# A decayed cumulative sum of x @ w: half of w's first quarter goes to GpSimd's queue, other first parts, and a float32 warm-up

## The chip, the cores and the metric

The kernel runs on one core of a Trainium2 chip. The metric is the device time of one launch in microseconds; lower is better. A core has TensorE (PE, matrix products), VectorE (DVE), ScalarE (ACT), GpSimd (POOL) and SyncE (SP), each with its own program, and 16 DMA engines that carry the transfers which SP, ACT and POOL issue.

## The reference

x has 16 batches of 2048 steps and 1024 features, w is 1024 x 1024, decay has 1024 values, all float32:

```python
xw = x @ w
out[:, 0, :] = xw[:, 0, :]
for t in range(1, S):
    out[:, t, :] = decay[None, :] * out[:, t - 1, :] + xw[:, t, :]
```

## The kernel before

**Tiling.** x is cut into 64 chunks of 512 steps (TL), four to a batch. A chunk is loaded by four DMAs, one for each quarter of the features (`load`, L105); each goes to 32 partitions, and GpSimd's queue turns float32 into bfloat16 on the way. A chunk has 16 blocks of 32 steps (NJ); a DMA may load some of the blocks only. VectorE transposes 32 x 32 blocks of pairs of bfloat16 (`turn`, L115, from `xb` to `xw`), so that the features lie on the partitions and each pair of neighbouring features is interleaved; ScalarE or VectorE pull the pairs apart (`part`, L123, to `xt`). Products can read the pairs straight from `xw` or the copies in `xt`. A product (L131) takes 128 features (k = 0 to 7) and 128 output columns (n = 0 to 7). Even k are the even rows of w (e = 0), odd k the odd ones (e = 1). The result in PSUM is scanned along the steps by VectorE (L229, or L210 on pairs that ScalarE and GpSimd have combined), transposed back (L266) and stored by SP (L290).

**Order.** Every engine's program follows the order of the lines, since each instruction is pinned. An agenda written by hand names deeds by letters; the string under -99 is the start, which the change touches:

- `M0` to `M3` (`load_half`): the loads of chunk 0's two parts and chunk 1's two parts. `cuts` says how many blocks a part has: chunk 0 has 9 and 7 (H is 8), chunk 1 has 8 and 8.
- `load_w` (L307): w is loaded in quarters (h: half of the columns, e: even or odd rows), each by four DMAs, one for each 32 partitions. Quarter (0, 0) goes in float32 over SP's and ACT's queues before all else; `U0` to `U2` (`load_part`) send the others over GpSimd's queue as bfloat16. They land in two `ot` tiles that are used for storing only later.
- `W` on VectorE, `w` on ScalarE (`settle`, L314): the copies of w into `wsb`, four for each quarter: 0 to 3 of (0, 0), 4 to 7 of (0, 1), and so on.
- `E` (transposes of a part, in four pieces), `F` and `G` (pulling the pairs apart on VectorE and ScalarE), `D` (decay's columns).
- `K0` to `K3` (`spin_on`, L348): warm-up products that wait for x. ScalarE copies one value of each quarter of x's first part into a gate matrix, and TensorE then multiplies with it.

**TensorE's start.** After a memset of `idle` it makes 22 products of zeros in bfloat16 (L332, 128 x 512), then 3, 3, 3 and 1 products with the four gates. Then come the products of chunk 0, part by part, four n at a time, even k from `xw` first, then odd k from `xt`; then those of chunk 1, its first blocks and then the rest; then whole chunks.

**GpSimd's queue.** Eight DMAs can be on their way at a time: each issue waits for the landing of the one eight before it. Order of the issues: `M0`, `U0`, `M1`, `M2`, `M3`, `U1`, `U2`, then chunk 2 and 3 of x (the deeds `L`). GpSimd also makes additions (L205, L254) between issues.

The lines for the start, as far as words don't tell them:

```python
    load_w((nc.sync, nc.scalar), 0, 0)
    pin(nc.vector.memset(idle, 0.0))
    ...
    spin(22, idle[:, 0:128])
    H = NJ // 2
    cuts = (((0, H + 1), (H + 1, NJ)), ((0, H), (H, NJ)))
    ...
    def spin_on(q):
        pin(nc.scalar.copy(out=gates[q][quad(q), 0:1], in_=xb_of[0][quad(q), 0, 0:1]))
        spin(3 if q < NQ - 1 else 1, gates[q])
```

Of the kernel before, what the change touches and what calls it, by code (L numbers as in the profile page):

```python
# [9 lines left out]
FP32 = mybir.dt.float32  # L10
BF16 = mybir.dt.bfloat16
# [3 lines left out]
def _ap(ap_obj: bass.AP, new_ap, extra_offset=0):  # L15
    return dataclasses.replace(
        ap_obj,
        ap=[list(p) for p in new_ap],
        offset=ap_obj.offset + extra_offset,
    )  # L20
# [5 lines left out]
def kernel(  # L26
# [26 lines left out]
    nc = tc.nc  # L53
    pin = tc.keep_in_program_order
    B, S, D = x.shape
    assert w.shape == (D, D)

    NQ = 4
    P = 32
    CQ = D // NQ  # L60
    K = CQ // P
    M = K // 2
    TL = 512
    NJ = TL // P
    NC = S // TL
    R = K // 2
    CH = D // 2
    CR = CH // NQ

    const = ctx.enter_context(tc.tile_pool(name="const", bufs=1))  # L70
# [5 lines left out]
    def ring(pool, name, count, shape, dtype=FP32):  # L76
        i = turns[name] = turns.get(name, -1) + 1
        return pool.tile(shape, dtype, name=f"{name}{i % count}")

    def quad(q):  # L80
        return slice(q * P, (q + 1) * P)
# [12 lines left out]
    def ot_tile(nj):  # L94
        return ring(sb, "ot", 4, [128, nj, CR])

    xb_of = {}
    xw_of = {}
    xt_of = {}
# [25 lines left out]
    def matmul(ps, n, k, xt, t0=0, t1=TL, start=0, pairs=None):  # L125
        if pairs is None:
            rhs = xt[:, k // 2, k % 2, t0:t1]
        else:
            rhs = pairs[:, k // 2, t0 // P:t1 // P, :, k % 2].rearrange("p j i -> p (j i)")
        lhs = wsb[:, k, n].rearrange("p q i -> p (q i)")  # L130
        pin(nc.tensor.matmul(  # L131
            out=ps[:, t0:t1] if ps.shape[1] >= t1 else ps,
            lhsT=lhs,
            rhs=rhs,
            start=(k == 0 and t0 == start),
            stop=(k == K - 1),
        ))
# [3 lines left out]
    class Tile:  # L141
# [45 lines left out]
        def copy(self):  # L187
            self.xs = sb.tile([128, 2 * TL], FP32, name=f"xs{self.lot % 3}")[:, 0:self.T]
            size = self.T // len(self.parts())
            for i, ps in enumerate(self.parts()):  # L190
                pin(nc.scalar.copy(out=self.xs[:, i * size:(i + 1) * size], in_=ps))  # L191
# [82 lines left out]
    class Outlet:  # L274
# [8 lines left out]
        def store(self, b, t0):  # L283
# [4 lines left out]
            for j in range(0, self.nj, nj):  # L288
# [8 lines left out]

    room = [ot_tile(2 * NJ).rearrange("p j c -> p (j c)") for _ in range(2)]
    size = M * CH
    stage = {(0, 0): room[0][:, 0:size],  # L300
             (0, 1): room[0][:, size:size * 3 // 2].bitcast(BF16),
             (1, 0): room[1][:, 0:size // 2].bitcast(BF16),
             (1, 1): room[1][:, size // 2:size].bitcast(BF16)}

    def load_w(queues, h, e):
        for i, q in enumerate((0, 2, 1, 3)):
            pin(queues[i % len(queues)].dma_start(  # L307
                out=stage[h, e][quad(q)].rearrange("p (m d) -> p m d", m=M),
                in_=_ap(w, [[2 * D, P], [2 * P * D, M], [1, CH]],
                        (q * CQ + e) * D + h * CH)))  # L310

    def settle(h, e, m, copy):
        src = stage[h, e][:, m * CH:(m + 1) * CH]
        pin(copy(out=wcols[:, 2 * m + e, h],  # L314
                 in_=src.rearrange("p (q r i) -> p q r i", q=NQ, r=R)))

    idle = const.tile([128, TL], BF16, name="idle")
    spare = ring(psp, "spare", 1, [128, TL])
    rows = const.tile([128, 2, P], FP32, name="rows")
    touch = const.tile([128, 1], BF16, name="touch")  # L320
    load_w((nc.sync, nc.scalar), 0, 0)
    pin(nc.vector.memset(idle, 0.0))  # L322
    pin(nc.vector.memset(rows, 0.0))
    pin(nc.scalar.copy(out=touch, in_=idle[:, 0:1]))

    gates = [const.tile([128, 128], BF16, name=f"gate{q}") for q in range(NQ)]
    for gate in gates:
        pin(nc.vector.memset(gate, 0.0))

    def spin(count, by):  # L330
        for _ in range(count):
            pin(nc.tensor.matmul(out=spare, lhsT=by, rhs=idle, start=True, stop=True))  # L332

    spin(22, idle[:, 0:128])
    H = NJ // 2
    cuts = (((0, H + 1), (H + 1, NJ)), ((0, H), (H, NJ)))
    for q in range(NQ):
        pin(nc.sync.dma_start(
            out=rows[q * P:q * P + R],
            in_=_ap(decay, [[P, R], [CH, 2], [1, P]], q * CR)))  # L340
# [4 lines left out]
            load(i // 2, q, *cuts[i // 2][i % 2])  # L345

    def spin_on(q):
        pin(nc.scalar.copy(out=gates[q][quad(q), 0:1], in_=xb_of[0][quad(q), 0, 0:1]))  # L348
        spin(3 if q < NQ - 1 else 1, gates[q])

    def load_part(i):
        load_w((nc.gpsimd,), *((0, 1), (1, 0), (1, 1))[i])

    def part_one(i, copy):
        part(i // 8, copy, i % 4, i % 4 + 1, *cuts[i // 8][i // 4 % 2])
# [65 lines left out]
    def turn_and_load(c):  # L421
# [38 lines left out]
        "L": lambda i: load(*loads.pop(0)) if loads else None,  # L460
    }
    agenda = {
        -99: "M0 U0 M1 M2 M3 U1 U2 w0 W1 w2 W3 K0 K1 K2 K3 E0 E1 G0 E2 G1 E3 F2 G3 W4 w5 W6 W7 D E4 E5 G4 E6 G5 E7 F6 G7 E8 E9 G8 E10 G9 E11 F10 G11 E12 L E13 G12 L E14 G13 E15 L F14 G15",
        0: "p0 z0 W8 W9 W10 W11",
        1: "g0",
        2: "L S1 L",
# [89 lines left out]
    for step, (g, n) in enumerate(slots):  # L556
        T = TL * len(g)
        left = step - len(slots)
        if n % R == 0:
            ns, nj = range(n, n + R), T // P  # L560
            if left == -2 * R:
                outlets = [Outlet(ns, H, half) for half in range(2)]
            else:
                pieces = 1 if left < -7 * R else 2 if left < -6 * R else nj // H
                outlets = [Outlet(ns, nj, pieces=pieces)]
        if left == -R:
            outlets = []
        if step == 0:
            heads = [ring(psp, "ps", 3, [128, T]) for _ in range(3)]
            firsts = [ps[:, 0:TL] for ps in heads] + [spares[0]]  # L570
            seconds = [ps[:, TL:T] for ps in heads] + [spares[1]]
            for j0, j1 in cuts[0]:
                for e in range(2):
                    for k in range(e, K, 2):
                        for i in range(R):
                            matmul(firsts[i], i, k, xt_of[0], j0 * P, j1 * P, j0 * P,
                                   pairs=None if e else xw_of[0])
            for k0 in range(0, K, 2):
                for i in range(R):
                    for k in (k0, k0 + 1):  # L580
                        matmul(seconds[i], i, k, xt_of[1], 0, H * P,
                               pairs=xw_of[1] if k0 < 4 else None)
            for i in range(R):
                for k in range(K):
                    matmul(seconds[i], i, k, xt_of[1], H * P, TL, H * P,
                           pairs=xw_of[1] if i < 2 else None)
        if step < R:
            ps = heads[n] if n < 3 else tuple(spares)
        else:
            if step == K + 1:  # L590
                ps = nexts
            elif len(g) == 2 or n % R < 3:
                ps = ring(psp, "ps", 3, [128, T])
            else:
                ps = ring(psp, "spare", 1, [128, TL])
            todo = [(k, l) for k in range(K) for l in range(len(g))]
            if step < K:
                todo.sort(key=lambda kl: kl[0] % 2)
            elif step == K:
                todo = []  # L600
                nexts = (ring(psp, "spare", 1, [128, TL]), ring(psp, "ps", 3, [128, T])[:, TL:T])
                for l in range(len(g)):
                    for i, one in enumerate((ps[:, l * TL:(l + 1) * TL], nexts[l])):
                        for k in range(K):
                            matmul(one, n + i, k, xt_of.get(g[l]),
                                   pairs=xw_of[g[l]] if l or not i and k >= M else None)
            elif step == K + 1:
                todo = []
            if left == -1:
                ps = tuple(both[:, t:t + TL // 2] for t, both in zip(  # L610
                    (0, TL // 2), (ps, ring(psp, "ps", 3, [128, TL]))))
                blocks += [bank("spare1", 1), bank("ps", 3)]
                for t, half in zip((0, TL // 2), ps):
                    for k in range(K):
                        matmul(half, n, k, xt_of[g[0]], t, t + TL // 2, t)
                    if not t:
                        cross((1,), (0, 1))
                todo = []
            for k, l in todo:
                matmul(ps[:, l * TL:(l + 1) * TL], n, k, xt_of[g[l]])  # L620
        tiles.append(Tile(g, n, ps, outlets))
        do = agenda.get(step, agenda.get(left) if left >= -20 else None)
        if do is None:
            do = usual(step)
        else:
            do = do.split()
            if left == -20:
                do = rest(step) + do
        perform(do)
# [29 lines left out]
```

## Time and profile before

| what | value |
|---|---|
| median of 3 runs | 905.64 us (904.32 to 905.7) |
| the profiled execution | 905.1 us, of which the span of instructions is 903.3 us |
| PE, DVE, ACT, POOL busy | 99%, 91%, 76%, 73% of the span |
| first warm-up product, first real product | 1.20 us, 10.61 us |
| last product begins | 898.62 us |
| clock granted to TensorE | 1.00 in the record |

The times of a trace are microseconds from the start of its span. A row of a timeline gives start, length, engine, line, operation, tiles (out<-in) and count, and in brackets the idle time of the engine before it with what ended it. PEld is TensorE's loading of weights, which overlaps with products. Products overlap in their ends too, so what one costs is read from the distance of starts: 0.216 us for 512 columns at full clock.

### The profile page before, as it was taken

To read this page: it belongs to the slowest core of one execution; us is meant where nothing else is said; L and a number is where in the kernel's file an instruction comes from. 1 tells how busy PE (TensorE), PEld (TensorE's weight loads), DVE (VectorE), ACT (ScalarE), POOL (GpSimd) and SP (SyncE) were. 2 spreads that over 40 slices of the span, in tenths; PEclk is the share of its full clock that TensorE was granted. 3 is DMA by queue.
4 is the path that set the end of the run, shared out by engine and by line. 5 is a ranking of instruction groups with operands and counts; after the bars stand their busy time and mean duration, and the time that the engine had idled before them with its cause. 6 is when DMAs were issued, how large, how long until landed. Compare 5 with 4: busy or idle time off the path is not lost.

```text
span 903.3 us, 12163 instructions
## 1 busy us (share of the span) xinstructions
PE 896.9 (99%) x4216; PEld 412.8 (46%) x4216; DVE 824.2 (91%) x632; ACT 685.9 (76%) x957; POOL 657.1 (73%) x755
## 2 busy tenths in 40 slices
PE   9999999999999999999999999999999999999998
PEld 5444444444444444444444444444444444444444
DVE  4899998998999999999998999999999999999998
ACT  4899867877877877878778778777787787787743
POOL 7978678877767778777677687777777776876632
PEclk9999999999999999999999999999999999999999
DMA  9999999999999999999999999999999999999858
GB/s 193 184 215 215 223 244 208 215 229 232 248 239 251 253 241 246 250 258 249 241 237 226 222 231 226 232 229 227 233 227 226 233 231 222 227 230 214 184 143 232
DMA packets 403182, 204.77 MB, mean 227 GB/s; under 512 B 9392, under 2 KB 402096, under 8 KB 403120
## 3 DMA queue, kind: packets, MB, share of 16 engines
q1 hardware_dynamic: 265808, 134.77, 60.9%
q0 software_dynamic: 137024, 68.70, 56.4%
q8 instruction: 33, 0.54, 0.2%
q10 hardware_dynamic: 288, 0.52, 0.2%
q14 instruction: 29, 0.24, 0.1%
HBM read 138.42 MB, written 134.22 MB: 302 GB/s over the span
## 4 chain that ended last, share of the span: by engine, by line
PE 92%; DMA 3%; DVE 2%; issue 1%; POOL 1%; ACT 0%; DVEq 0%; POOLq 0%; ACTq 0%
PE ps L131 91%; DMA xb<-in_x_dram 2%; POOL xb L105 1%; DMA ot<-in_w_dram 1%; PE spare L131 1%; DVE so L229 1%; DVE ot L266 0%; DVE so L210 0%; DVE xw L115 0%; POOL xs L205 0%; PE spare L392 0%; PE ps L392 0%; ACT h L171 0%; DVE h L401 0%; POOL so L199 0%
## 5 line engine op out<-in xcount | busy, mean ns | idle before, releaser
L131 PE MATMUL ps<-xt,wsb 128*128 128x512 bf16 (+1 forms) x4024 | 865.6, 378 | 0.4 <-DVE so L229 0.4
L131 PEld LDWEIGHTS <-wsb 128*128 128x128 bf16 x4168 | 407.3, 98 | 479.0 <-issue 1.7
L205 POOL TENSOR_TENSOR xs<-h,xs 128x512 f32<-128x512 f32 (+1 forms) x190 | 242.8, 1278 | 183.1 <-ACT h L171 84.6
L266 DVE STREAM_TRANSPOSE ot<-so 128x1024 f32<-128x1024 f32 (+2 forms) x264 | 300.1, 1175 | 5.7 <-DMA out_dram<-ot 3.6
L191 ACT COPY xs<-ps 128x1024 f32<-128x1024 f32 (+1 forms) x190 | 188.8, 994 | 145.2 <-PE ps L131 141.6
L254 POOL TENSOR_TENSOR so<-h,xs 128x512 f32<-128x512 f32 (+1 forms) x190 | 241.1, 1271 | 48.0 <-ACT h L171 28.1
L123 ACT COPY xt<-xw 128x2048 bf16<-128x2048 bf16 (+3 forms) x136 | 242.1, 1788 | 8.9 <-DVE xw L115 8.9
L105 POOL DMA_DIRECT2D xb<-in_x_dram x264 | 174.2, 661 | 6.7 <-DMA xb<-in_x_dram 3.1
L171 ACT ACTIVATE h<-so,dec 128x512 f32<-128x512 f32 (+1 forms) x190 | 145.3, 765 | 37.3 <-DVE so L210 34.0
L115 DVE STREAM_TRANSPOSE xw<-xb 128x2048 f32<-128x2048 f32 (+3 forms) x78 | 147.4, 1902 | 8.8 <-DMA xb<-in_x_dram 8.8
L210 DVE TENSOR_TENSOR_SCAN so<-spare,keep,xs 128x512 f32<-128x512 f32 (+1 forms) x97 | 119.6, 1236 | 24.1 <-POOL xs L205 23.9
L210 DVE TENSOR_TENSOR_SCAN so<-spare,xs 128x512 f32<-128x512 f32 x93 | 113.2, 1219 | 26.4 <-POOL xs L205 23.5
L171 ACT ACTIVATE h<-ps,dec 128x512 f32<-128x512 f32 (+1 forms) x190 | 129.9, 683 | 0.0
L229 DVE TENSOR_TENSOR_SCAN so<-dec,ps 128x1024 f32<-128x1024 f32 x34 | 76.8, 2261 | 1.0 <-ACT h L171 1.0
L229 DVE TENSOR_TENSOR_SCAN so<-dec,keep,ps 128x1024 f32<-128x1024 f32 (+1 forms) x35 | 75.9, 2169 | 0.0
L258 ACT COPY keep<-so 128x1 f32<-128x1 f32 x136 | 25.3, 189 | 9.6 <-DVE so L229 9.0
L201 ACT COPY so<-keep 128x1 f32<-128x1 f32 x97 | 18.4, 191 | 2.7 <-DVE ot L266 2.5
L131 PE MATMUL ps<-xw,wsb 128*128 128x256 bf16 (+3 forms) x72 | 12.3, 306 | 0.4 <-DVE xw L115 0.4
L131 PE MATMUL spare<-xt,wsb 128*128 128x512 bf16 (+3 forms) x60 | 12.6, 330 | 0.0
L199 POOL MEMSET so<- 128x1 f32 x93 | 10.6, 116 | 0.6 <-DVE ot L266 0.6
L332 PE MATMUL spare<-idle 128*128 128x512 bf16 x22 | 7.4, 515 | 1.2 <-DVE idle L322 1.2
L307 POOL DMA_DIRECT2D ot<-in_w_dram x12 | 6.5, 545 | 1.0 <-issue 0.4
(39 smaller groups left out, 37.9 us busy)
## 6 DMA issues: line engine op xcount, KB each, us to landing
out_dram<-ot SPq DMA_DIRECT2D x236, 512.0 KB, 11.1
xb<-in_x_dram POOLq DMA_DIRECT2D x248, 256.0 KB, 7.9
out_dram<-ot SPq DMA_DIRECT2D x56, 128.0 KB, 2.6
out_dram<-ot SPq DMA_DIRECT2D x8, 256.0 KB, 4.0
ot<-in_w_dram POOLq DMA_DIRECT2D x12, 128.0 KB, 6.1
xb<-in_x_dram POOLq DMA_DIRECT2D x8, 128.0 KB, 4.8
out_dram<-xb SPq DMA_DIRECT2D x3, 256.0 KB
xb<-in_x_dram POOLq DMA_DIRECT2D x4, 144.0 KB, 6.2
```

Of the source, the lines that this page charges most:

```text
L105: pin(nc.gpsimd.dma_start(out=xb_of[c][quad(q), j0:j1], in_=_ap(x, [[D, P], [P * D, j1 - j0], [1, CQ]], (b * S + t0 + j0 * P) * D + q * CQ)))
L115: pin(nc.vector.transpose(out=dst.rearrange("p (m j i) -> p j m i", m=M, i=P)[:, j0:j1, m0:m1], in_=src.rearrange("p (j m c) -> p j m c", ...
L123: pin(copy(out=xt_of[c][:, m0:m1, :, j0 * P:j1 * P], in_=src))
L131: pin(nc.tensor.matmul(out=ps[:, t0:t1] if ps.shape[1] >= t1 else ps, lhsT=lhs, rhs=rhs, start=(k == 0 and t0 == start), stop=(k == K - 1),))
L171: pin(nc.scalar.activation(out=h[:, i * size:(i + 1) * size], in_=src, func=mybir.ActivationFunctionType.Copy, scale=dec[:, self.n:self.n ...
L191: pin(nc.scalar.copy(out=self.xs[:, i * size:(i + 1) * size], in_=ps))
L205: pin(nc.gpsimd.tensor_tensor(out=odds, in0=self.g, in1=odds, op=ALU.add))
L210: pin(nc.vector.tensor_tensor_scan(out=so[:, 3:T + 2:2], data0=squares[-1][:, n:n + 1].to_broadcast([128, T // 2]), data1=self.xs[:, 1:T:2 ...
L229: pin(nc.vector.tensor_tensor_scan(out=so[:, t + 2:t + 2 + size], data0=dec[:, n:n + 1].to_broadcast([128, size]), data1=ps, initial=befor ...
L254: pin(nc.gpsimd.tensor_tensor(out=self.so[:, 2:T + 2:2], in0=self.h, in1=self.xs[:, 0:T:2], op=ALU.add))
L258: pin(nc.scalar.copy(out=self.keep, in_=self.so[:, self.T + 1:self.T + 2]))
L266: pin(nc.vector.transpose(out=outlet.ot[:, :, c0:c0 + P], in_=self.so[:, 2 + t0:2 + t0 + nj * P].rearrange("p (i t) -> p i t", t=P)))
```

## The change

Five things change, all of them before TensorE's steady stream.

- w's quarter (0, 0) is divided. The first two of its four row groups (m = 0 and 1) go in float32 over SP and ACT, as the whole quarter did; the other two (m = 2 and 3) go as bfloat16 over GpSimd's queue in four DMAs of 64 KB, ahead of `M0`. `U0` is now this half, and `U1` to `U3` are the former `U0` to `U2`.
- `cuts`: chunk 0 is loaded, transposed and multiplied in parts of 10 and 6 blocks (before 9 and 7), chunk 1 in parts of 7 and 9 (before 8 and 8). The products of chunk 1 use the same bound (`Q`).
- The order of issues on GpSimd's queue becomes `U0 M0 U1 M1 M2 M3 U2 U3`.
- The 22 bfloat16 warm-up products become 4 products of float32 (128 x 512) on a tile `wide` that VectorE clears.
- Of the gated products only one stays, with the last quarter of x's first part (`K3`).

```diff
-    stage = {(0, 0): room[0][:, 0:size],
-             (0, 1): room[0][:, size:size * 3 // 2].bitcast(BF16),
+    stage = {(0, 1): room[0][:, size:size * 3 // 2].bitcast(BF16),
              (1, 0): room[1][:, 0:size // 2].bitcast(BF16),
              (1, 1): room[1][:, size // 2:size].bitcast(BF16)}
 
-    def load_w(queues, h, e):
+    lead = {0: room[0][:, 0:2 * CH], 2: room[0][:, 2 * CH:3 * CH].bitcast(BF16)}
+
+    def load_w(queues, to, h, e, m0=0, m1=M):
         for i, q in enumerate((0, 2, 1, 3)):
             pin(queues[i % len(queues)].dma_start(
-                out=stage[h, e][quad(q)].rearrange("p (m d) -> p m d", m=M),
-                in_=_ap(w, [[2 * D, P], [2 * P * D, M], [1, CH]],
-                        (q * CQ + e) * D + h * CH)))
+                out=to[quad(q)].rearrange("p (m d) -> p m d", d=CH),
+                in_=_ap(w, [[2 * D, P], [2 * P * D, m1 - m0], [1, CH]],
+                        (q * CQ + 2 * P * m0 + e) * D + h * CH)))
 
     def settle(h, e, m, copy):
-        src = stage[h, e][:, m * CH:(m + 1) * CH]
+        if h or e:
+            src = stage[h, e][:, m * CH:(m + 1) * CH]
+        else:
+            src = lead[m // 2 * 2][:, m % 2 * CH:(m % 2 + 1) * CH]
...
-    idle = const.tile([128, TL], BF16, name="idle")
+    wide = const.tile([128, TL], FP32, name="wide")
+    idle = wide[:, 0:TL // 2].bitcast(BF16)
...
-    load_w((nc.sync, nc.scalar), 0, 0)
-    pin(nc.vector.memset(idle, 0.0))
+    load_w((nc.sync, nc.scalar), lead[0], 0, 0, 0, 2)
+    pin(nc.vector.memset(wide, 0.0))
...
-    gates = [const.tile([128, 128], BF16, name=f"gate{q}") for q in range(NQ)]
-    for gate in gates:
-        pin(nc.vector.memset(gate, 0.0))
-
-    def spin(count, by):
+    gate = const.tile([128, 128], BF16, name="gate")
+    pin(nc.vector.memset(gate, 0.0))
+
+    def spin(count, by, on):
         for _ in range(count):
-            pin(nc.tensor.matmul(out=spare, lhsT=by, rhs=idle, start=True, stop=True))
-
-    spin(22, idle[:, 0:128])
+            pin(nc.tensor.matmul(out=spare, lhsT=by, rhs=on, start=True, stop=True))
+
+    spin(4, wide[:, 0:128], wide)
     H = NJ // 2
-    cuts = (((0, H + 1), (H + 1, NJ)), ((0, H), (H, NJ)))
+    cuts = (((0, H + 2), (H + 2, NJ)), ((0, H - 1), (H - 1, NJ)))
...
     def spin_on(q):
-        pin(nc.scalar.copy(out=gates[q][quad(q), 0:1], in_=xb_of[0][quad(q), 0, 0:1]))
-        spin(3 if q < NQ - 1 else 1, gates[q])
+        pin(nc.scalar.copy(out=gate[quad(q), 0:1], in_=xb_of[0][quad(q), 0, 0:1]))
+        spin(1, gate, idle)
 
     def load_part(i):
-        load_w((nc.gpsimd,), *((0, 1), (1, 0), (1, 1))[i])
+        if i:
+            load_w((nc.gpsimd,), stage[i // 2, i % 2], i // 2, i % 2)
+        else:
+            load_w((nc.gpsimd,), lead[2], 0, 0, 2)
...
-        -99: "M0 U0 M1 M2 M3 U1 U2 w0 W1 w2 W3 K0 K1 K2 K3 E0 E1 G0 E2 G1 E3 F2 G3 W4 w5 W6 W7 D E4 E5 G4 E6 G5 E7 F6 G7 E8 E9 G8 E10 G9 E11 F10 G11 E12 L E13 G12 L E14 G13 E15 L F14 G15",
+        -99: "U0 M0 U1 M1 M2 M3 U2 U3 w0 W1 w2 W3 K3 E0 E1 G0 E2 G1 E3 F2 G3 W4 w5 W6 W7 D E4 E5 G4 E6 G5 E7 F6 G7 E8 E9 G8 E10 G9 E11 F10 G11 E12 L E13 G12 L E14 G13 E15 L F14 G15",
...
+            Q = cuts[1][0][1] * P
             for k0 in range(0, K, 2):
                 for i in range(R):
                     for k in (k0, k0 + 1):
-                        matmul(seconds[i], i, k, xt_of[1], 0, H * P,
+                        matmul(seconds[i], i, k, xt_of[1], 0, Q,
                                pairs=xw_of[1] if k0 < 4 else None)
             for i in range(R):
                 for k in range(K):
-                    matmul(seconds[i], i, k, xt_of[1], H * P, TL, H * P,
+                    matmul(seconds[i], i, k, xt_of[1], Q, TL, Q,
                            pairs=xw_of[1] if i < 2 else None)
```

## The prediction

> **What bounds the kernel now.** I read the page's busy shares first, then the chain of work that ended last, then the timeline of each engine over the first 70 us, because the diff touches nothing that runs later.
>
> ```profile
> PE 896.9 (99%) x4216; PEld 412.8 (46%) x4216; DVE 824.2 (91%) x632; ACT 685.9 (76%) x957; POOL 657.1 (73%) x755
> PE 92%; DMA 3%; DVE 2%; issue 1%; POOL 1%; ACT 0%; DVEq 0%; POOLq 0%; ACTq 0%
> ```
>
> TensorE is busy 99% of 903.3 us, so the change can only move what comes before its steady stream. That stream has few holes: the timeline of PE (start, length, what; idle time and its releaser in brackets) shows these.
>
> ```profile
> 1.20 7.42 PE L332 MATMUL spare<-idle 128*128 128x512 bf16 x22 [1.20 <-DVE idle L322]
> 8.45 2.32 PE L332 MATMUL spare<-idle,gate 128*128 128x512 bf16 x10
> 10.61 0.55 PE L131 MATMUL ps<-xw,wsb 128*128 128x288 bf16 x3
> ...
> 15.31 0.46 PE L131 MATMUL ps<-xw,wsb 128*128 128x224 bf16 x3 [0.38 <-DVE xw L115]
> ...
> 25.56 14.64 PE L131 MATMUL ps<-xt,wsb 128*128 128x512 bf16 x67
> ...
> 67.98 0.38 PE L131 MATMUL ps<-xt,wsb 128*128 128x512 bf16 x1 [0.45 <-DVE so L229]
> ```
>
> Warm-up products fill 1.20 to 10.61 without a hole, real products start at 10.61, wait once at 15.31, are a solid stream from 25.56, wait once more at 67.98, and never after. So two things set the end: when PE gets through its first parts, and when VectorE's chain releases PE at 67.98. That chain is DVE back to back from 39.83, after this wait for chunk 3 of x:
>
> ```profile
> 9.77 1.56 DVE L115 STREAM_TRANSPOSE xw<-xb 128x288 f32<-128x288 f32 x4 [2.05 <-DMA xb<-in_x_dram]
> ...
> 12.45 0.70 DVE L314 COPY wsb<-ot 128x512 bf16<-128x512 bf16 x3 [0.78 <-DMA ot<-in_w_dram]
> ...
> 14.85 1.29 DVE L115 STREAM_TRANSPOSE xw<-xb 128x224 f32<-128x224 f32 x4 [1.14 <-DMA xb<-in_x_dram]
> ...
> 17.55 1.42 DVE L115 STREAM_TRANSPOSE xw<-xb 128x256 f32<-128x256 f32 x4 [1.11 <-DMA xb<-in_x_dram]
> ...
> 20.27 1.43 DVE L115 STREAM_TRANSPOSE xw<-xb 128x256 f32<-128x256 f32 x4 [0.98 <-DMA xb<-in_x_dram]
> ...
> 39.83 2.31 DVE L115 STREAM_TRANSPOSE xw<-xb 128x2048 f32<-128x2048 f32 x1 [1.38 <-DMA xb<-in_x_dram]
> ```
>
> Each row begins when a load has landed: x's four first parts at about 9.66, 14.74, 17.44 and 20.16. They come over GpSimd's queue (q0), which POOL's timeline shows being fed, while the DMA view of 0 to 5.2 us holds no q0 packet at all:
>
> ```profile
> 1.31 2.55 POOL L105 DMA_DIRECT2D xb<-in_x_dram  x4 [0.86 <-POOLq L643]
> 3.85 2.16 POOL L307 DMA_DIRECT2D ot<-in_w_dram  x4
> ```
> ```profile
> q1 hardware_dynamic: 286, 0.52, 38.2%
> q10 hardware_dynamic: 243, 0.46, 26.6%
> ```
>
> The same view to 5.5 us holds 40 packets of q0. So x, issued at 1.31, starts to flow at 5.2: 3.9 us later. Once more the queue starts from empty: x issued at 131.95 has no packet up to 135.2 (3.3 us). Float32 w on SP's and ACT's queues (q1, q10), issued at 0.75, flows from between 1.5 and 2.0.
>
> **The change part by part.**
>
> *Queues.* SP and ACT issue the same four loads at half size (0.5 MB instead of 1 MB); the decay rows behind them on SP lose nothing. GpSimd gets four more issues, ahead of x: 4 x 0.54 = 2.2 us, so x's first issue moves from 1.31 to 3.5 and its fourth ends at 5.95 instead of 3.86. Their data, 4 x 64 KB as bf16 = 262 KB, go through q0 first: at the 203 GB/s of the stretch 20 to 24, where w alone flows, 1.3 us. The half taken off SP and ACT returns little, since it flowed while q0 was still empty.
>
> *x's first part lands.* w flows from 5.2 to 6.5. x is ready at 3.5 + 3.3 = 6.8. Ten blocks are 4 x 160 KB = 655 KB; at the 193 GB/s of 12 to 15, 3.4 us: 10.2. In the trace the same sum (5.2 + 590 KB / 193 = 8.3) falls short of the landing by 1.4 us; about 0.5 of that is float32 w still flowing beside it to 6.5, which is now gone, and 0.9 is spread over the 16 engines. I take 0.6 of 0.3 to 0.9: 10.8 (10.5 to 11.1), against 9.66. From landing to the first real product goes the 320-column transpose (0.50, scaled from 288) and 0.2 around it: 11.5, against 10.61. The old 10.61 was not x's limit: transposes began at 9.77, and the queue of gated warm-up products ended only at 10.61. That backlog, some 0.3 us, goes.
>
> *First part, 320 columns.* 16 products from xw at 0.142 (0.128 each at 288) end at 13.8. The next 16 need w's odd rows, which follow x on q0: 10.2 + 524 KB / 203 + 0.6 = 13.4, then 0.5 of copying (as 12.33 to 12.80): 13.9, so the old wait of 0.16 stays. 16 x 0.136: 16.1. Before it was 14.93.
>
> *Second part, 192 columns.* It lands at 12.8 + 393 KB / 193 + 0.6 = 15.4, or 15.7 by its issue, since its fourth issue waits for x's fourth landing at 10.8 and takes 4.8 as that of 9.93 did. Plus 0.6: 16.0 to 16.3. The wait before 15.31 all but goes; 32 products cost 0.083 (columns alone) to 0.100 (what 224 columns take with weight loads); I take 0.09: 19.0, against 18.44.
>
> *Chunk 1, 7 and 9 blocks instead of 8 and 8.* Landings 17.8 and 20.9, transposed 18.4 and 21.6, both before PE comes (19.0 and 22.1). 32 x 0.098 + 32 x 0.124 = 7.1, as before: 26.1 against 25.56. PE is **0.5 us late**.
>
> *Chunk 3.* Everything on q0 after the first parts is 0.75 later (20.9 against 20.16). x's chunk 2 is issued at 22.50 when w's third quarter has landed (22.2), and chunks 2 and 3 then flow one behind the other to 39.7. All shifts by about 0.7, and with it the release at 67.98. PE's 0.5 disappears in that wait. Bounds: 0.0, if the landing at 22.2, which came 2 us after x's, now follows closer, and 1.1.
>
> *Warm-up.* Out go 22 plain and 10 gated products, 3 copies on ACT (0.19 each), 3 memsets; in come 4 float32 products, 1 gated one and a memset of 512 instead of 256 words (0.27 more, PE starts at 1.45). None is on the path if PE is at full clock when x is there. The old rows show the clock: 12 products in 5.09 us (0.427 each), then 0.216 from 6.27. The nearest float32 row is at the end,
>
> ```profile
> L392 PE MATMUL ps<-ident,so 128*128 128x128 f32 x8 | 1.4, 273 | 0.0
> ```
>
> whose starts are 0.11 apart for 128 columns, twice a bf16 column. At twice, four products take 3.5 us at half clock; at four times 6.8. I take four, since a transpose only passes values through. Then PE is busy from 1.45 to 7.3 (clock up at 6.27) or 8.3, and empty to the gated product at 11.0: 2.7 to 3.7 us. The gated product (copy 0.19, product 0.22) ends before the first transpose.
>
> The Trainium skill (TensorE: Matmul & The Clock Gate, Part 1) says the clock rises after about 3.4 us of activity in a free-running window and falls after as long without; its table (Why this matters for your kernels) asks for no gap over about 3 us. The old rows agree with the rise; no run here shows a fall. By that rule the gap is at the edge, and a window empty from end to end rarely fits into it, which leaves my sum alone; where it fits, rival one comes.
>
> Sum: profiled execution 905.1 + 0.7 = 905.8. The runs' median, 905.64, is 0.5 above that execution, so I forecast 906.3.
>
> **Rivals.** *One, a cold array.* If the products keep PE busy too briefly (two passes: empty from 5.0 on), or the empty stretch lowers the clock, real products start at half speed. For: from 8.3 to 11 nothing runs. Against: 6.8 us exceed the 5.1 that raised the clock. Price, with the old cold stretch of 5.1 us from 11.5: half of it, 2.5, is lost; PE 3.0 late at 26, less the 0.75 of waits that swallow it (0.61 at 67, 0.14 about 46 to 50, both start to start): +2.3, 908.0. It exceeds 0.2% when the cold stretch is over 4.1 us.
>
> *Two, q0 was held back by float32 w.* If q0's late start is the crowd of q1 and q10 packets up to 5.2, halving those lets it start at 3.4: x lands at 3.4 + 1.3 + 3.4 + 0.9 = 9.0, PE starts at 9.7, waits nowhere, and everything is 1.4 earlier: 904.2. Against: the 3.3 us at 131.95, though stores flowed there too, and x's issue at 3.5.
>
> The Trainium skill (DMA: Bandwidth & Descriptors, Latency and other measured facts) gives about 1 us to the first byte from GpSimd. The rows show 3.9 and 3.3, and the measurement decides; by the page, rival two would be right.
>
> **How the numbers follow.** My case 0.56, cold 0.32, early x 0.12. About 0.2% (1.8 us) is what a measurement of this kernel tells from no change. My case: same 0.48, slower 0.06, faster 0.02. Cold: slower 0.22, same 0.10. Early x: faster 0.06, same 0.06. In all faster 0.08, same 0.64, slower 0.28. Range: from rival two's 904.2 to the cold case with a slightly longer stretch, 908.5.
>
> **What would show it.** Right: no q0 packet before 5; transposes of 320 columns beginning near 10.9; PE's first real product near 11.5 at 0.14 apart; no wait before the 192-column products; the 67.98 wait near 68.7; float32 products ending between 7.3 and 8.3. Wrong: real products 0.28 apart (cold), the first transpose before 9.8 (early x), or a new wait for w's odd rows of over 0.5.

## The result and the profile after

The changed kernel takes **907.62 us** (median of 7 runs, 906.77 to 909.48), the kernel before 904.57 us (median of 7, 904.32 to 905.7). The ratio is 1.0032 with a 95% interval of 1.0022 to 1.0042: slower by 3.05 us. The three runs behind the 905.64 us of the table ahead are the first three of before's seven; with the other four its median is 1.07 lower. The profiled execution of after took 906.77 us (span 904.7 us). It is the fastest of its seven, while the one of before (905.1, span 903.3) is among the slower, so the two traces differ by 1.4 us only. The traces show how it happened; how much each part costs is read from medians.

The page says what it said before, with a little less of the chain in waiting for loads and a little more in PE:

```profile
PE 894.1 (99%) x4193; PEld 411.6 (45%) x4193; DVE 823.8 (91%) x629; ACT 685.8 (76%) x954; POOL 659.9 (73%) x759
PE 98%; DMA 1%; POOL 0%; issue 0%; DVE 0%; ACT 0%; ACTq 0%; POOLq 0%
```

The timeline of PE over the first 28 us of after answers to the one shown of before:

```profile
1.46 5.43 PE L336 MATMUL spare<-wide 128*128 128x512 f32 x8 [1.46 <-DVE wide L327]
11.62 0.47 PE L336 MATMUL spare<-wide,gate 128*128 128x512 bf16 x1 [4.73 <-ACT gate L352]
11.98 0.96 PE L131 MATMUL ps<-xw,wsb 128*128 128x320 bf16 x3
...
13.01 1.00 PE L131 MATMUL ps<-xw,wsb 128*128 128x320 bf16 x3
...
17.92 0.42 PE L131 MATMUL ps<-xw,wsb 128*128 128x192 bf16 x3
...
27.73 0.59 PE L131 MATMUL ps<-xt,wsb 128*128 128x512 bf16 x2
```

The float32 products are done at 6.89 (each has two rows, hence x8), and PE then has nothing for 4.73 us. Real products begin at 11.98 instead of 10.61. Four of them start in 13.01 - 11.98 = 1.03 us, some 0.26 each; from 15.14 on it is 0.14. The stream of whole chunks begins at 27.73 instead of 25.56, 2.17 us late. The three stretches of 3.41 us from 4.97 to 15.21 give the reason (busy time of PE, PEld, DVE, ACT and POOL, each with its number of instructions, then the granted clock, DMA share and GB/s):

```profile
4.97:8.38 3.41, 1.92 (x5) 0.57 (x3) 0.72 (x2) 1.24 (x2) 3.24 (x6) 1.00 1.08 130
8.38:11.80 3.42, 0.18 (x1) 0.11 (x2) 0.38 (x1) 0.19 (x1) 1.91 (x4) 1.00 1.24 168
11.80:15.21 3.41, 3.41 (x14) 1.75 (x13) 2.80 (x11) 2.60 (x4) 3.27 (x6) 0.50 1.37 194
```

PE is busy for 0.18 of 3.42 us in the second stretch, and the third is granted half the clock, just when x is there. In before the clock rose once, at 6.27, and stayed. VectorE's timeline shows the loads, each row beginning when one has landed:

```profile
11.42 1.69 DVE L115 STREAM_TRANSPOSE xw<-xb 128x320 f32<-128x320 f32 x4 [4.42 <-DMA xb<-in_x_dram]
...
16.08 1.16 DVE L115 STREAM_TRANSPOSE xw<-xb 128x192 f32<-128x192 f32 x4 [0.79 <-DMA xb<-in_x_dram]
...
18.47 1.29 DVE L115 STREAM_TRANSPOSE xw<-xb 128x224 f32<-128x224 f32 x4 [0.99 <-DMA xb<-in_x_dram]
...
22.23 1.56 DVE L115 STREAM_TRANSPOSE xw<-xb 128x288 f32<-128x288 f32 x4 [2.20 <-DMA xb<-in_x_dram]
```

Against before the first part is 1.65 us later (11.42 against 9.77), the last of the four 1.96 (22.23 against 20.27). Of the 2.17 us at the start of the whole-chunk stream, two later waits of before swallow 0.76 (0.61 at 67, 0.15 between 46 and 50, start to start; after waits at neither), and 2.17 - 0.76 = 1.41 is the difference of the spans.

### The profile page after: what moved, and what is told of

Same layout as the page of the kernel before. It is cut to its first block, busy times and chain, and to the rows that moved or that the text cites. A ratio compares the mean times of both kernels' runs of the same rounds, so it can differ in the third digit from the quotient of the medians.

```text
span 904.7 us, 12116 instructions
## 1 busy us (share of the span) xinstructions
PE 894.1 (99%) x4193; PEld 411.6 (45%) x4193; DVE 823.8 (91%) x629; ACT 685.8 (76%) x954; POOL 659.9 (73%) x759
## 4 chain that ended last, share of the span: by engine, by line
PE 98%; DMA 1%; POOL 0%; issue 0%; DVE 0%; ACT 0%; ACTq 0%; POOLq 0%
PE ps L131 97%; PE spare L131 1%; DMA xb<-in_x_dram 1%; POOL ot L308 0%; POOL xb L105 0%; PE spare L399 0%; PE ps L399 0%; DVE h L408 0%; PE spare L336 0%; ACT gate L352 0%; ACTq L352 0%; POOLq L651 0%
## 5 line engine op out<-in xcount | busy, mean ns | idle before, releaser
L123 ACT COPY xt<-xw 128x2048 bf16<-128x2048 bf16 (+4 forms) x136 | 242.3, 1790 | 8.3 <-DVE xw L115 8.3
L115 DVE STREAM_TRANSPOSE xw<-xb 128x2048 f32<-128x2048 f32 (+4 forms) x78 | 147.3, 1900 | 11.0 <-DMA xb<-in_x_dram 11.0
L131 PE MATMUL ps<-xw,wsb 128*128 128x512 bf16 (+4 forms) x72 | 13.6, 327 | 0.0
L131 PE MATMUL spare<-xt,wsb 128*128 128x512 bf16 (+5 forms) x60 | 12.6, 330 | 0.0
L308 POOL DMA_DIRECT2D ot<-in_w_dram x16 | 8.8, 555 | 2.2 <-DMA xb<-in_x_dram 1.2
L336 PE MATMUL spare<-wide 128*128 128x512 f32 x8 | 5.4, 838 | 1.5 <-DVE wide L327 1.5
```

Source lines behind the costliest of these rows:

```text
L115: pin(nc.vector.transpose(out=dst.rearrange("p (m j i) -> p j m i", m=M, i=P)[:, j0:j1, m0:m1], in_=src.rearrange("p (j m c) -> p j m c", ...
L123: pin(copy(out=xt_of[c][:, m0:m1, :, j0 * P:j1 * P], in_=src))
L131: pin(nc.tensor.matmul(out=ps[:, t0:t1] if ps.shape[1] >= t1 else ps, lhsT=lhs, rhs=rhs, start=(k == 0 and t0 == start), stop=(k == K - 1),))
```

## The experiments

Theory A ("late x", or "bytes"): the 262 KB of w that now go ahead of x on GpSimd's queue delay every later load on it. Theory B ("cold array", the prediction's rival one): the short warm-up leaves PE empty, the clock falls, and real products start at half speed. The part sizes could add to either. All times are medians. e1 to e4, e5 to e8, and e9 and e10 ran on a chip each, every time beside the kernel before, which stood at 904.49 with e1 to e8 and at 904.56 with e9 and e10. "Clock" is the mean granted clock of whole executions, over all runs; of after's seven runs all have 0.995 to 0.998, of before's beside the experiments all 0.999 or 1.000. One stretch of 3.41 us at half clock takes 0.0019 off it (half of 3.41 in 905). It also loses up to 0.0013 at the end in these traces, when PE has nothing left (e10 has 0.50 from 900.5 on). So 0.999 goes without a fall at the start, and 0.995 and 0.996 need, by this estimate, more than one cold stretch.

| kernel | what it is | us (lowest to highest, runs) | ratio to before | clock |
|---|---|---|---|---|
| e1 | after, old warm-up | 906.35 (905.8 to 907.75, 11) | 1.0023 [1.0014, 1.0031] | 0.999 to 1.000 |
| e5 | after, eight float32 products | 906.25 (905.55 to 907.64, 10) | 1.0020 [1.0011, 1.0029] | 0.999 to 1.000 |
| e2 | before, new warm-up | 905.34 (904.44 to 907.27, 11) | 1.0010 [1.0001, 1.0019] | 0.995 to 1.000 |
| e3 | before, new queue | 905.96 (905.47 to 906.48, 11) | 1.0015 [1.0006, 1.0024] | 0.999 to 1.000 |
| e9 | before, a quarter instead of half | 905.38 (904.94 to 905.86, 10) | 1.0010 [1.0001, 1.0020] | 0.999 to 1.000 |
| e6 | before, new queue, behind x's first part | 906.52 (905.49 to 907.31, 10) | 1.0022 [1.0013, 1.0032] | 0.998 to 1.000 |
| e4 | before, all new sizes | 905.04 (904.09 to 907.21, 11) | 1.0008 [0.9999, 1.0017] | 0.999 to 1.000 |
| e7 | before, chunk 0 in 10 and 6 | 904.37 (904.05 to 905.57, 10) | 0.9999 [0.9990, 1.0009] | 0.999 to 1.000 |
| e8 | before, chunk 1 in 7 and 9 | 904.39 (904.07 to 906.01, 10) | 1.0001 [0.9992, 1.0011] | 0.999 to 1.000 |
| e10 | before, new sizes, seven float32 products | 904.83 (904.26 to 905.43, 10) | 1.0004 [0.9995, 1.0013] | 0.999 to 1.000 |

**The warm-up: e1, e2, e5.** e1 is after with the warm-up of before:

```diff
-    spin(4, wide[:, 0:128], wide)
+    spin(22, idle[:, 0:128])
...
-        pin(nc.scalar.copy(out=gate[quad(q), 0:1], in_=xb_of[0][quad(q), 0, 0:1]))
-        spin(1, gate, idle)
+        pin(nc.scalar.copy(out=gates[q][quad(q), 0:1], in_=xb_of[0][quad(q), 0, 0:1]))
+        spin(3 if q < NQ - 1 else 1, gates[q])
```

> The changed kernel with the old warm-up (22 products of zeros in bfloat16, then 3, 3, 3 and 1 gated ones). Theory 'cold array': the loss is mostly the half clock over TensorE's first products, which comes because TensorE stood empty from 6.89 to 11.62; with the old warm-up the empty time is under 1.5 us (22 and the gates end by 11.7), the granted clock stays 1.00 from its rise on, the first products are 0.14 apart, and the time is 0 to +1.0 us against the kernel before. Rival 'late x': x's first part landing at 11.3 instead of 9.7 is what costs; then it stays at +2.5 to +3.5 us with the old warm-up too.

It came between the two: 1.86 us slower than before, some 1.2 better than after. So both theories seem to hold a share. PE's timeline:

```profile
8.83 0.82 PE L336 MATMUL spare<-idle,gate 128*128 128x512 bf16 x3 [0.71 <-ACT gate L352]
9.84 2.15 PE L336 MATMUL spare<-idle,gate 128*128 128x512 bf16 x7 [0.20 <-ACT gate L352]
11.97 0.58 PE L131 MATMUL ps<-xw,wsb 128*128 128x320 bf16 x3
...
22.76 2.51 PE L131 MATMUL ps<-xw,wsb 128*128 128x288 bf16 x16 [0.21 <-DVE xw L115]
...
27.06 1.24 PE L131 MATMUL ps<-xt,wsb 128*128 128x512 bf16 x4
```

Real products begin at 11.97, as in after (11.98), but at 0.14 apart, and the clock is 0.999 or more in every run. x is as late as in after (transposed from 11.40 against 11.42); what differs in the traces is the clock.

e2 does the reverse, the new warm-up alone, with one gated product in place of ten:

```diff
-    spin(22, idle[:, 0:128])
+    spin(4, wide[:, 0:128], wide)
```

> The kernel before with the new warm-up alone (four float32 products, one gated product). 'Cold array' through the length of the empty stretch: products end at 6.9 to 8.3, x lands at 9.7, so TensorE stands empty for 1.7 to 3 us, too short for a whole 3.4 us stretch of it; clock stays 1.00, time within 0.5 us of the kernel before. Rival 'float32 products do not keep the clock up': it falls here too, time +1.5 to +2.5 us. 'Late x': x is not late here, so 0.

Measured: 0.85 us slower, between its two expectations, and in two groups by the clock. Six of the eleven runs have a clock of 0.995 to 0.997 (median 905.7), five of 0.999 or more (904.76). The profiled one is of the second kind: its float32 products end at 7.28, PE is empty for 3.31 us up to 10.60, and the clock holds:

```profile
1.46 5.82 PE L332 MATMUL spare<-wide 128*128 128x512 f32 x8 [1.46 <-DVE wide L323]
10.60 0.39 PE L332 MATMUL spare<-wide,gate 128*128 128x512 bf16 x1 [3.31 <-ACT gate L348]
```

So without the new queue, the short warm-up lowers the clock in about half of the executions; with it, in all seven of after. The lengths 3.31 and 4.73 us are of one execution each; how long PE was empty in the others isn't known.

e5 lengthens after's warm-up and leaves all else:

```diff
-    spin(4, wide[:, 0:128], wide)
+    spin(8, wide[:, 0:128], wide)
```

> The changed kernel with eight float32 products instead of four, nothing else. They end at 10.3 to 11.7, so TensorE is empty for under 1.2 us before x. 'Cold array': every run shows a granted clock of 0.999 or 1.0 and the time is that of the changed kernel with the old warm-up, +1.3 to +2.2 us against the kernel before (906.4), 1 us better than the changed kernel. Rival 'the float32 products themselves or the single gate cost it': clock may be whole, but the time stays near +3.

It is 1.3 us better than after (1.0020 against 1.0032 of before), and the same as e1. PE's timeline has an empty stretch of 1.98 us (under 1.2 was expected), and the clock is 0.999 or more in every run:

```profile
1.46 8.67 PE L336 MATMUL spare<-wide 128*128 128x512 f32 x16 [1.46 <-DVE wide L327]
12.12 0.39 PE L336 MATMUL spare<-wide,gate 128*128 128x512 bf16 x1 [1.98 <-ACT gate L352]
```

That float32 products replace bfloat16 ones costs nothing that can be told; that there are only four costs some 1.3 us. The intervals of e1 and e5 overlap that of after, so the size is rough; that after loses clock and these two don't is seen in every run.

Not all of this loss is in the traces. The time of a run less its span of instructions is 1.73 to 1.91 us in every run of the kernel before beside the experiments and of the nine other experiments. In after it is 1.78 to 2.83 and in e2 1.74 to 2.98, and these two are the kernels with four float32 products. In means, after takes 907.63 us with a span of 905.43, e1 906.57 with 904.79, e5 906.45 with 904.64: of the 1.1 to 1.2 us between them 0.6 to 0.8 lie in the span and 0.4 outside. e2's two largest, 2.74 and 2.98, have a clock of 1.000 and spans of 902.6 and 902.5, as short as those of before (902.7 in the median). What fills the time outside the span isn't shown. So the short warm-up is shown as the cause of the whole; the cold array, which lies in the span, can account for that part only.

**The queue: e3, e9, e6.** e3 is before with half of the quarter on GpSimd's queue, ahead of x, at the old sizes and with the old warm-up:

```diff
-    load_w((nc.sync, nc.scalar), 0, 0)
+    load_w((nc.sync, nc.scalar), lead[0], 0, 0, 0, 2)
...
-        -99: "M0 U0 M1 M2 M3 U1 U2 w0 ...
+        -99: "U0 M0 U1 M1 M2 M3 U2 U3 w0 ...
```

> The kernel before with the new queue order alone (half of w's first quarter on GpSimd's queue ahead of x); parts of 9 and 7, 8 and 8 blocks, old warm-up. 'Cold array': x's first part lands near 10.9 (a tenth less of it than in the changed kernel), TensorE's gated products wait for it for less than 1.5 us, clock 1.00, +0.5 to +1.2 us. 'Late x': +2.5 to +3.5 us. GpSimd's queue should begin to flow near 3.7 as in the changed kernel, not at 5.2.

It is 1.47 us slower, more than the first theory expected and less than the second, with every run between 905.47 and 906.48 and no loss of clock. VectorE's timeline shows each load of x later by about the same:

```profile
11.14 1.56 DVE L115 STREAM_TRANSPOSE xw<-xb 128x288 f32<-128x288 f32 x4 [3.93 <-DMA xb<-in_x_dram]
...
16.12 1.29 DVE L115 STREAM_TRANSPOSE xw<-xb 128x224 f32<-128x224 f32 x4 [1.12 <-DMA xb<-in_x_dram]
...
18.85 1.43 DVE L115 STREAM_TRANSPOSE xw<-xb 128x256 f32<-128x256 f32 x4 [1.09 <-DMA xb<-in_x_dram]
...
21.60 1.42 DVE L115 STREAM_TRANSPOSE xw<-xb 128x256 f32<-128x256 f32 x4 [1.02 <-DMA xb<-in_x_dram]
...
41.20 2.31 DVE L115 STREAM_TRANSPOSE xw<-xb 128x2048 f32<-128x2048 f32 x1 [1.37 <-DMA xb<-in_x_dram]
```

Against the rows of before: 1.37, 1.27, 1.30, 1.33 and, for chunk 3, 1.37 later. 262 KB at 203 GB/s take 1.29 us. PE's wait for VectorE's chain, at 67.98 in before, is still there, 1.37 later:

```profile
69.35 10.95 PE L131 MATMUL ps<-xt,wsb 128*128 128x512 bf16 x49 [0.45 <-DVE so L229]
```

So what is put ahead on this queue delays all that follows by about the transfer time of its bytes, and reaches the end through the chain that the prediction named. The landings of one execution are not those of a kernel, though: with the loads as before, x's first part, of the same size, was transposed from 10.40 in e2's trace and from 10.67 in e8's, against 9.77. The reading rests on five rows that agree, and on the times.

e9 moves one of the four row groups (131 KB) instead of two, in four DMAs as before, to tell bytes from issues:

```diff
-    lead = {0: room[0][:, 0:2 * CH], 2: room[0][:, 2 * CH:3 * CH].bitcast(BF16)}
+    lead = {0: room[0][:, 0:3 * CH], 3: room[0][:, 3 * CH:3 * CH + CH // 2].bitcast(BF16)}
...
-    load_w((nc.sync, nc.scalar), lead[0], 0, 0, 0, 2)
+    load_w((nc.sync, nc.scalar), lead[0], 0, 0, 0, 3)
```

(The lines taken out are e3's.)

> The kernel before with a fourth of w's first quarter (one row group, 131 KB) on GpSimd's queue ahead of x, in four DMAs as in the changed kernel, three fourths staying on SP and ACT; old sizes, old warm-up. Half of it moved made every later landing 1.3 us later and the time +1.5 us. If the bytes on GpSimd's queue set this, landings are 0.65 us later and the time +0.5 to +0.9 us; if the four more issues ahead of x (2.2 us of GpSimd) set it, landings stay 1.3 us later and the time +1.2 to +1.6 us.

The time, 0.82 us slower, is about half of e3's, as bytes say; the intervals of the two overlap, though. Its trace does not side with the bytes:

```profile
9.78 1.56 DVE L115 STREAM_TRANSPOSE xw<-xb 128x288 f32<-128x288 f32 x4 [1.87 <-DMA xb<-in_x_dram]
...
15.98 1.29 DVE L115 STREAM_TRANSPOSE xw<-xb 128x224 f32<-128x224 f32 x4 [1.13 <-DMA xb<-in_x_dram]
```

The first part of x is not later at all (9.78, against 9.77), but the three parts behind it are 1.1 later (15.98, 18.69 and 21.40), nearer to the 1.3 that it expected of the issues than to the 0.65 of 131 KB at 203 GB/s. So bytes and issues are not told apart; the times alone speak for bytes.

e6 keeps the 262 KB on GpSimd's queue but puts them behind x's first part:

```diff
-        -99: "U0 M0 U1 M1 M2 M3 U2 U3 w0 W1 w2 W3 K0 K1 K2 K3 E0 E1 G0 ...
+        -99: "M0 U0 U1 M1 M2 M3 U2 U3 w0 W1 K0 K1 K2 K3 E0 E1 w2 W3 G0 ...
```

(The line taken out is e3's.)

> The kernel before with half of w's first quarter on GpSimd's queue, but behind x's first part instead of ahead of it (and the copies of that half behind the first two transposes); old sizes, old warm-up. If the place ahead of x is what makes x late, x lands before 9.7 and the time is -0.5 to +0.4 us. If the 262 KB more on GpSimd's queue are (everything behind them moves), +0.8 to +1.5 us. It also tells why the queue began at 3.5 in place of 5.2: if float32 w on the other queues held it back, x flows from 3.5 here; if x's larger first transfer takes longer to begin (36 rows for each of 32 partitions against 8), from 5.

It came out above both of its ranges, the worst of the three: 2.03 us slower. x's first part did land earlier than ever, at about 8.83 (9.64 in before). But the fourth issue for w's odd rows now stood behind x's fourth landing, came at 9.12, and its data landed at about 13.81. PE's timeline has a new wait:

```profile
14.28 0.54 PE L131 MATMUL ps<-xt,wsb 128*128 128x288 bf16 x3 [2.08 <-DVE wsb L318]
```

Behind this wait the clock fell here too (half from 14.90 to 18.31; the stretches are shown at the end), and x's later parts are 2.13 to 2.15 later than in before (16.98, 19.70 and 22.40), more than the 1.29 of the bytes. So putting w behind x saves nothing, since something that PE needs still comes behind it. How the 2.03 us divide between bytes, order of issues and clock isn't shown.

**The sizes: e4, e7, e8, e10.** e4 sets all four sizes as after has them, e7 only chunk 0's, e8 only chunk 1's; e10 has e4's sizes and a float32 warm-up of seven products with one gated product.

```diff
-    cuts = (((0, H + 1), (H + 1, NJ)), ((0, H), (H, NJ)))
+    cuts = (((0, H + 2), (H + 2, NJ)), ((0, H - 1), (H - 1, NJ)))
```

> The kernel before with the new sizes of the parts alone (10 and 6 blocks, 7 and 9). Both theories: the sizes are not the cause. x's first part lands 0.35 us later (64 KB more at 193 GB/s), the second part's wait at 15.31 goes; -0.5 to +0.4 us, clock 1.00.

> The kernel before with parts of 10 and 6 blocks of chunk 0 alone. The new sizes together gave +0.55 us in the median, and between -0.4 and +2.7 by run, at full clock. If the larger first part is the cause: +0.3 to +1.0 us and a spread of over 1.5 us here, none with the other cut.

> The kernel before with parts of 7 and 9 blocks of chunk 1 alone. If the late, larger last part (9 blocks) is what stalls TensorE near 22 us in some runs: +0.3 to +1.0 us and a spread of over 1.5 us here, and none with the cut of chunk 0.

> The kernel before with the new sizes and seven float32 products with one gated product; the queues as before. They end at 9.5 to 11.1 us, x's first part lands near 10.2, so TensorE is never empty for over 1 us. 'Cold array': clock 0.999 or 1.0 in every run, and with the sizes at nothing the time is within 0.6 us of the kernel before. If the float32 warm-up costs something besides the empty stretch, over +0.8 us.

e4 came out 0.55 us slower, a little above what was expected, with an interval that includes no change and single runs up to 907.21. Each half by itself costs nothing that can be told (e7, e8), and both with another warm-up nothing that can be told (e10, 0.27). e4's spread was not seen again and stays unexplained. e10 also shows the float32 warm-up harmless when it is long enough: PE is empty for 0.38 us only.

```profile
1.46 8.51 PE L332 MATMUL spare<-wide 128*128 128x512 f32 x14 [1.46 <-DVE wide L323]
10.36 0.39 PE L332 MATMUL spare<-wide,gate 128*128 128x512 bf16 x1 [0.38 <-ACT gate L348]
```

Beside the new queue the sizes may cost something. In the traces of e1 and e5 PE waits 0.21 and 0.80 us for x's last part, which has nine blocks. The timelines of e3, with the old sizes, and of e4 and e10, with the old queue, show no such wait.

In sum: the queue 1.5 us (e3), the short warm-up 1.2 to 1.3 us (after against e1 and e5), the sizes 0 to 0.5. That makes 2.7 to 3.3, and 3.05 was measured. No version was faster than the kernel before beyond its interval.

## Why the prediction was right or wrong

The forecast was 906.3 us, with 0.64 on a change of less than 0.2%; the outcome was slower by 0.32%, to which it gave 0.28. That 907.62 lies in the range of 904.2 to 908.5 is in part luck. The range was built around 905.64, the median of three runs, and the kernel before stands at 904.57. As a change, the forecast was +0.7 and the range went from -1.4 to +2.9 us; +3.05 is outside. Rival one, with a weight of 0.32, came true, on top of a queue cost twice as large as forecast.

**The step that failed first: "Everything on q0 after the first parts is 0.75 later."** That was 1.29 us of transfer, from which the prediction took 0.5 because float32 w would no longer flow beside. e3's trace gives 1.27 to 1.37 for every part, so the credit did not show. After's own windows show why the first part took so long: all queues together moved 141 and 124 GB/s between 7 and 8 and 8 and 9 us, where the kernel before moved 178 and 198. What holds the flow down there was not found. And this chain does not set the end in after: PE comes so late that no wait is left at 67, and its own lateness, which the prediction let vanish in that wait, is what counts.

**The second: the warm-up as an edit on no path.** That a float32 product takes as long as four bfloat16 ones was right: its starts lie 1.71 us apart before the clock rises and 0.86 after, and a bfloat16 product of 512 columns takes 0.427 and 0.216. But the prediction took the rise from the old trace, at 6.27. It came at 4.97, so the last products ran twice as fast and ended at 6.89 instead of 7.3 to 8.3. And x landed at about 11.30 instead of 10.8. Both errors lengthened the empty stretch, from 2.7 to 3.7 us as forecast to 4.73.

**Rival one** had its mechanism and its sign ("0.28 apart") right: 12 products at 0.267. Its price, 2.3 us for a cold stretch of 5.1 us, was too high: the stretch lasted 3.41 us, from 11.80 to 15.21, of which the products fill 3.2. After's trace is 1.36 behind e1's at chunk 1 (20.62 against 19.26) and only 0.67 where whole chunks begin (27.73 against 27.06), because e1, with the faster start, then waits for a part of x that lands no sooner (0.21 at 22.76, and more within the 16 products behind it). The medians differ by 1.2. The three runs of after with a clock of 0.995 or 0.996 have its longest spans (905.5, 905.8 and 907.7), which fits more than one cold stretch, but no trace of them was kept; and part of the difference lies outside the span, as said.

**Rival two** (q0 held back by float32 w; price -1.4) was right in its mechanism, as far as these runs go, and wrong in its gain. The first packet of GpSimd's queue comes at 3.64 in after, and at 3.47 in e6, where it is x itself, against 5.2 before. The prediction's "no q0 packet before 5" is thus refuted, and so is its 3.3 us from x's issue to its flow (3.47 - 1.31 = 2.16 in e6). In after this brings x nothing, because w's 262 KB are what flows first.

**Right:** the chain from chunk 3's landing to the release at 67.98 (e3: 69.35); no wait ahead of the 192-column products, and their cost (0.086 and 0.082, taken as 0.09); nothing lost by the sizes alone as far as can be told; PE's lateness going into the later waits, 0.76 of 2.17.

The Trainium skill (TensorE: Matmul & The Clock Gate, Why this matters for your kernels) asks for no gap over about 3 us, because one idle window lowers the clock. The runs agree: the kernel whose trace has an empty stretch of 4.73 us lost clock in seven of seven runs, the one with 3.31 us in six of eleven, the one with 1.98 us in none of ten. The prediction had this rule beside its row and still put the gap at its edge, by a sum whose two errors pointed the same way.

## What to carry to other kernels

A warm-up has to reach until the data is there: its length follows from the landing of the first load, with a margin for that load's own delay, and not from the time that the clock needs to rise. Loads put ahead on the queue that orders all later ones cost about the transfer time of their bytes here, even though they started earlier and another queue was relieved. Before an edit is costed at nothing, add up what the other edits of the same change do to its cover: here the later x widened the very hole that the shorter warm-up left. And state a range as a change against the kernel before: three runs had put its median 1.07 us too high.

## What the runs showed of the hardware

- The clock also fell after a stretch in which PE was not empty. In e6 the stretch 11.49 to 14.90 (ahead of the fall at 14.90) had PE busy 39% of the time; in e2 a stretch with 44%, 5.76 to 9.17, was followed by full clock. The changes of clock lie 3.41 us apart in after (11.80 and 15.21) and in e6 (14.90 and 18.31).

```profile
11.49:14.90 3.41, 1.33 (x11) 0.80 (x10) 1.17 (x6) 1.74 (x3) 2.96 (x5) 1.00 1.17 142
14.90:18.31 3.41, 3.41 (x18) 2.21 (x16) 1.58 (x7) 0.88 (x2) 2.79 (x5) 0.50 1.37 173
```

```profile
5.76:9.17 3.41, 1.52 (x4) 0.38 (x2) 0.76 (x2) 1.14 (x2) 0.87 (x2) 1.00 1.42 199
```

The first two lines are e6's, the last is e2's, in the columns of the stretches above.

- When GpSimd's queue begins to move, after an issue at about 1.3, went with what the other two queues carry: 5.05 to 5.42 in the six traces with 1 MB of float32 on them, 4.39 with three quarters of that (e9), 3.44 to 3.64 with half (e1, e3, e5, e6, after).
